# Strassen's seven products for gate and up in a two-layer decoder kernel

## The chip, the cores and the metric

One core of a Trainium2 chip runs the whole program. The time is device microseconds of one execution, the median of the runs. TensorE (PE) multiplies, VectorE (DVE) and ScalarE (ACT) work elementwise, GpSimd (POOL) does small scalars, and SyncE (SP) issues the loads.

## The reference, cut to what matters

Two layers on 256 tokens of width 1024, all in 32-bit floats. Each layer has four sublayers: a gated unit, a mixer with two attentions, a second gated unit, and a gated embedding. The change touches the gated units, four in all:

```python
D_MODEL, SEQ, DEPTH, D_FF = 1024, 256, 2, 2816

def swiglu(x, w_gate, w_up, w_down):
    return (jax.nn.silu(x @ w_gate) * (x @ w_up)) @ w_down

for i in range(DEPTH):
    f = swiglu(rmsnorm(h, g[0]), ffn_gate[i, 0], ffn_up[i, 0], ffn_down[i, 0])
    h = h + 0.5 * rmsnorm(f, g[1])
    # mixer, second gated unit, gated embedding
```

## The kernel before

Every 32-bit product is made of three TensorE matmuls: each operand is split into `hi + lo`, and `hi*hi`, `hi*lo`, `lo*hi` are summed in PSUM (`mm3`). The weight is the moving operand, 512 columns at a time; the 256 tokens are two tiles of 128 (`t`), and a block of their transpose (`xh`, `xl`, 128 x 128) is the stationary one.

`Weights` streams the weights in the order of use. SP loads 1 MB into one of four raw tiles (L131). `prepare` takes a half of it, a piece of 1024 elements per partition: ACT copies it into `hi` (L152), DVE subtracts to get `lo` (L153). The pieces lie in slots: eight, and in the gated units two more that the mixer otherwise uses. `need` prepares a piece on the spot if it isn't there; `finish` gives its slot back when the last matmul that reads it has been emitted. When a raw tile's last piece is split, the next load is emitted.

The engines' queues are in the order in which the program emits. A phase is a generator that yields after every three matmuls or so; `run` puts in the splits (`W.tick`) and other work at the steps that a table, `PLAN`, has for the phase.

A gated unit (`ffn`) goes over `CHUNKS`, six stretches of its 2816 hidden columns, 512 wide and one of 256. In each: gate and up for both tiles (`gate`, `up`; 24 matmuls each at 512 columns), silu on ACT (L448), the product on DVE (L453), transposes and split of the hidden tile (`hid_t`, L398 to L402), and the product with `w_down` (`down`, L479), which sums over all chunks in four PSUM banks (`accs`). The factor of the norm before (`rx`) is put in at silu and product. In the first chunk, what the sublayer before has left over (the rest of its norm and the transposes of x, `pend`) lies between the matmuls; the last chunk ends with the norm after (`begin_post`, `post`).

The bank pool `mm` has four banks, in rotation, for gate, up and the transposes.

Of the kernel before, what the change touches and what calls it, by code (L numbers as in the profile page):

```python
# [17 lines left out]
P = 128  # L18
D = 1024
# [17 lines left out]
NRAW = 4  # L37
CHUNKS = [(0, 512), (512, 512), (1024, 256), (1280, 512), (1792, 512), (2304, 512)]
# [58 lines left out]
class Weights:  # L97
    """Streams the weights in the order of their use: one load per raw tile, which is then
    split into pieces hi + lo = w, each of 12 significant bits."""

    def __init__(self, nc, raw_pool, slots):
        """slots: pairs of (pool, tag, columns) for hi and lo; those of self.shut are taken by others."""
        self.nc, self.raw_pool, self.slots = nc, raw_pool, slots
        self.free = list(range(len(slots)))
        self.shut = set()
        self.slot = {}
        self.specs = []
        self.loads = []
        self.raw = {}
        self.got = {}  # L110
        self.next = 0
        self.next_load = 0

    def add(self, keys, src, a, n):
        load = len(self.loads)
        self.loads.append((src, a * len(keys), n))
        for i, key in enumerate(keys):
            self.specs.append((key, load, i, a, n, i == len(keys) - 1))

    def load_one(self):  # L120
        i = self.next_load
        if i >= len(self.loads):
            return
        src, a, n = self.loads[i]
        raw = self.raw_pool.tile([P, 2048], F32, tag="raw", name=f"raw{i}")
        view = raw[:, : a * n].rearrange("p (a n) -> p a n", n=n)
        if i == 0:
            for j in range(0, a, a // 2):
                self.nc.sync.dma_start(view[:, j : j + a // 2], src[:, j : j + a // 2])
        else:  # L130
            self.nc.sync.dma_start(view, src)  # L131
        self.raw[i] = view
        self.next_load += 1

    def pick(self):
        return next((i for i in self.free if i not in self.shut), None)

    def can(self):
        return self.next < len(self.specs) and self.pick() is not None

    def prepare(self):
        key, load, part, a, n, last = self.specs[self.next]
        while self.next_load <= load:
            self.load_one()
        raw = self.raw[load][:, part * a : (part + 1) * a, :]
        slot = self.pick()
        self.free.remove(slot)
# [3 lines left out]
        hv, lv = (v.rearrange("p (a n) -> p a n", n=n) for v in (hi, lo))  # L151
        self.nc.scalar.activation(hv, raw, AF.Copy)  # L152
        self.nc.vector.tensor_tensor(lv, raw, hv.bitcast(F32), op=ALU.subtract)  # L153
        self.got[key] = (hv, lv)
        self.next += 1
        if last:
            del self.raw[load]
            self.load_one()
# [4 lines left out]

    def need(self, key):
        while key not in self.got:
            assert self.can(), (key, self.specs[self.next])
            self.prepare()
        return self.got[key]

    def finish(self, key):  # L170
        self.free.append(self.slot.pop(key))
        self.free.sort()
# [3 lines left out]
def hybrid_block(ctx: ExitStack, tc: tile.TileContext, a, out):  # L176
# [53 lines left out]
    ones = const.tile([1, P], F32, name="ones")  # L230
    nc.gpsimd.memset(ones, 1.0)

# [1 line left out]
    slots = [((piece_pool, f"hi{i}", 1024), (piece_pool, f"lo{i}", 1024)) for i in range(NS)]  # L234
    slots += [((work, "kdt", 1024), (work, "grp", 1024)), ((work, "vm", T * H * VW), (work, "vd", T * H * VW))]
    W = Weights(nc, raw_pool, slots)
    for l in range(DEPTH):
        for f in range(2):
            if f == 1:
# [3 lines left out]
                def add_in(name, c0, n):  # L243
                    for j in range(2):
                        W.add([(l, name, 2 * j), (l, name, 2 * j + 1)], win[:, 4 * j : 4 * j + 4, c0 : c0 + n], 2, n)

                add_in("A", 0, ZA)
                add_in("dq", ZA, 512)
                W.add([(l, "qu", 0), (l, "qu", 1)], a["w_q_up"][l].rearrange("(k p) n -> p k n", p=P), 1, 768)
                W.add([(l, "kvu", 0)], a["w_kv_up"][l].rearrange("(k p) n -> p k n", p=P), 1, 1024)  # L250
                add_in("dk", ZA + 512, 512)
                add_in("dv", ZA + 1024, 512)
                for half in range(2):
                    for n in range(2):
                        W.add([(l, "wo", half, n, 0), (l, "wo", half, n, 1)],
                              wo[:, 4 * half : 4 * half + 4, n * 512 : (n + 1) * 512], 2, 512)
            wg = a["ffn_gate"][l, f].rearrange("(k p) n -> p k n", p=P)
            wu = a["ffn_up"][l, f].rearrange("(k p) n -> p k n", p=P)
            wd = a["ffn_down"][l, f].rearrange("(k p) n -> p k n", p=P)
            for c, (f0, w) in enumerate(CHUNKS):  # L260
                ka = 1024 // w
                for name, src in (("G", wg), ("U", wu)):
                    for j in range(KD // (2 * ka)):
                        W.add([(l, f, c, name, 2 * j), (l, f, c, name, 2 * j + 1)],
                              src[:, 2 * ka * j : 2 * ka * (j + 1), f0 : f0 + w], ka, w)
                for j in range(w // 256):
                    k0 = f0 // P + 2 * j
                    W.add([(l, f, c, "D", 2 * j), (l, f, c, "D", 2 * j + 1)], wd[:, k0 : k0 + 2, :], 1, 1024)
        gt = a["w_ple_gate"][l].rearrange("(k p) n -> p k n", p=P)
        for n in range(2):  # L270
            for j in range(2):
                W.add([(l, "gt", n, 2 * j), (l, "gt", n, 2 * j + 1)],
# [637 lines left out]
```

## Time and profile before

| | |
|---|---|
| median of 2 runs | 1053.22 us (1052.02 to 1054.42) |
| span of the profiled execution | 1052.4 us |
| PE busy | 1037.1 us, 5168 matmuls |
| DVE busy | 645.8 us, 819 instructions |
| ACT busy | 528.9 us, 744 instructions |
| POOL busy | 51.1 us, 123 instructions |
| bytes moved by DMA | 189.02 MB |

The profiled execution is known by its span, which lies 0.8 us below the median of the runs. Busy time is the time with at least one instruction of the engine under way; waits are listed as "engine line <- releaser: us in total, times, longest". A row of a group ends with its busy time, the mean ns of one, and the idle time before it with what ended it. In the timeline each row begins with start and length.

### The profile page before, as it was taken

How to read it: one execution, taken by the hardware profiler on the slowest of the kernel's cores; microseconds unless marked ns; L12 is line 12 of the kernel's file. 1: busy time of each engine (PE TensorE's matmuls, PEld its weight loads, DVE VectorE, ACT ScalarE, POOL GpSimd, SP SyncE). 2: the span in 40 equal slices, each digit the busy share in tenths (PEclk: the TensorE clock that was granted, in tenths of full speed). 3: DMA queues.
4: the chain of work that ended last, by engine and by line, in shares of the span. 5: the costliest groups of instructions: out<-in, count | busy, mean ns of one | idle time of the engine just before them, and what ended most of it. 6: DMA issues, size and time to landing. Idle time of an engine off the chain costs nothing.

```text
span 1052.4 us, 13069 instructions
## 1 busy us (share of the span) xinstructions
PE 1037.1 (99%) x5168; PEld 867.0 (82%) x5168; DVE 645.8 (61%) x819; ACT 528.9 (50%) x744; POOL 51.1 (5%) x123
## 2 busy tenths in 40 slices
PE   8999999999999999999999999999999999999997
PEld 5889888878888898888878888888888888988886
DVE  4765554778677455456776545557877864555474
ACT  5544443555556444444665444445564654444463
POOL 0000000210020000000110000002000200000011
PEclk9999999999999999999999999999999999999999
DMA  8864546364227564554547645455532575545601
GB/s 321 304 227 168 193 164 211 106 222 160 82 94 272 191 213 160 201 200 160 200 160 259 212 169 200 153 163 168 180 120 82 190 275 184 198 162 172 227 21 40
DMA packets 86158, 189.02 MB, mean 180 GB/s; under 512 B 3665, under 2 KB 15313, under 8 KB 86098
## 3 DMA queue, kind: packets, MB, share of 16 engines
q1 hardware_dynamic: 86098, 188.20, 52.0%
q8 instruction: 40, 0.66, 0.2%
q14 instruction: 20, 0.16, 0.0%
HBM read 187.13 MB, written 1.05 MB: 179 GB/s over the span
## 4 chain that ended last, share of the span: by engine, by line
PE 92%; DVE 3%; ACT 2%; DMA 1%; issue 1%; POOL 0%; SPq 0%; DVEq 0%; POOLq 0%; ACTq 0%
PE acc L479 23%; PE u L323 8%; PE u L321 8%; PE u L322 8%; PE g L321 7%; PE g L323 7%; PE g L322 7%; PE tp L398 3%; PE o L706 2%; PE sc L666 1%; DVE lo L153 1%; PE gt L323 1%; PE gt L322 1%; PE gt L321 1%; PE f L321 1%; PE f L323 1%
## 5 line engine op out<-in xcount | busy, mean ns | idle before, releaser
L153 DVE TENSOR_TENSOR lo<-raw,hi 128x1024 fp32r<-128x1024 f32 (+1 forms) x338 | 405.1, 1214 | 204.2 <-ACT hi L152 194.1
L152 ACT ACTIVATE hi<-raw 128x1024 fp32r<-128x1024 f32 (+1 forms) x338 | 347.2, 1049 | 170.9 <-PE u L323 79.3
L479 PE MATMUL acc<-hi,hid 128*128 128x512 f32 x704 | 201.5, 392 | 0.0
L479 PEld LDWEIGHTS acc<-hi,hid 128*128 128x128 f32 x704 | 131.7, 188 | 27.4
L321 PE MATMUL u<-hi,xh 128*128 128x512 f32 (+1 forms) x384 | 145.3, 379 | 0.0
L323 PE MATMUL u<-hi,xl 128*128 128x512 f32 (+1 forms) x384 | 143.2, 373 | 0.0
L322 PE MATMUL u<-lo,xh 128*128 128x512 f32 (+1 forms) x384 | 143.0, 372 | 0.0
L321 PE MATMUL g<-hi,xh 128*128 128x512 f32 (+1 forms) x360 | 135.0, 375 | 2.3 <-ACT xh L401 2.3
L323 PE MATMUL g<-hi,xl 128*128 128x512 f32 (+1 forms) x360 | 134.6, 374 | 0.0
L322 PE MATMUL g<-lo,xh 128*128 128x512 f32 (+1 forms) x360 | 134.5, 374 | 0.0
L479 PE MATMUL acc<-lo,hid 128*128 128x512 f32 x352 | 118.3, 395 | 0.0
L323 PEld LDWEIGHTS u<-hi,xl 128*128 128x128 f32 x384 | 72.3, 188 | 13.0
L322 PEld LDWEIGHTS u<-lo,xh 128*128 128x128 f32 x384 | 72.4, 188 | 12.1
L321 PEld LDWEIGHTS u<-hi,xh 128*128 128x128 f32 x384 | 72.3, 188 | 12.0
L321 PEld LDWEIGHTS g<-hi,xh 128*128 128x128 f32 x360 | 68.5, 190 | 14.4 <-ACT xh L401 2.7
L322 PEld LDWEIGHTS g<-lo,xh 128*128 128x128 f32 x360 | 68.5, 190 | 12.3 <-DVE lo L153 0.5
L323 PEld LDWEIGHTS g<-hi,xl 128*128 128x128 f32 x360 | 68.4, 190 | 12.4 <-DVE xl L402 0.6
L479 PEld LDWEIGHTS acc<-lo,hid 128*128 128x128 f32 x352 | 66.2, 188 | 13.2
L401 ACT ACTIVATE hid<-tp 128x512 fp32r<-128x512 f32 (+1 forms) x48 | 27.0, 563 | 95.6 <-PE tp L398 95.6
L453 DVE SCALAR_TENSOR_TENSOR hm<-u,rs,silu 128x512 f32<-128x512 f32 (+1 forms) x48 | 33.7, 703 | 65.1 <-PE u L323 65.1
L448 ACT ACTIVATE silu<-g,rs 128x512 f32<-128x512 f32 (+1 forms) x48 | 31.3, 652 | 81.3 <-PE g L323 81.2
L402 DVE TENSOR_TENSOR hid<-tp,hid 128x512 fp32r<-128x512 f32 (+1 forms) x48 | 31.0, 647 | 44.0 <-ACT hid L401 43.6
(216 smaller groups left out, 1195.0 us busy)
## 6 DMA issues: line engine op xcount, KB each, us to landing
raw<-in_ffn_up SPq DMA_DIRECT2D x44, 1024.0 KB, 5.1
raw<-in_ffn_down SPq DMA_DIRECT2D x44, 1024.0 KB, 5.0
raw<-in_ffn_gate SPq DMA_DIRECT2D x43, 1024.0 KB, 5.2
raw<-in_w_in SPq DMA_DIRECT2D x12, 1024.0 KB, 5.2
raw<-in_w_out SPq DMA_DIRECT2D x8, 1024.0 KB, 5.1
raw<-in_w_ple_gate SPq DMA_DIRECT2D x8, 1024.0 KB, 5.1
gain<-in_norm_gains SPq DMA_DIRECT2D x15, 512.0 KB, 4.0
raw<-in_w_in SPq DMA_DIRECT2D x4, 832.0 KB, 5.2
```

What stands on the lines that cost most here:

```text
L152: self.nc.scalar.activation(hv, raw, AF.Copy)
L153: self.nc.vector.tensor_tensor(lv, raw, hv.bitcast(F32), op=ALU.subtract)
L321: nc.tensor.matmul(ps, sh, wh, start=first, stop=False)
L322: nc.tensor.matmul(ps, sh, wl, start=False, stop=False)
L323: nc.tensor.matmul(ps, sl, wh, start=False, stop=last)
L398: nc.tensor.transpose(ps[:, j * P : (j + 1) * P], src[:, (b0 + j) * P : (b0 + j + 1) * P], ident)
L401: nc.scalar.activation(hv, v, AF.Copy)
L402: nc.vector.tensor_tensor(dl[:, k0 + b0 : k0 + b0 + nb, :], v, hv.bitcast(F32), op=ALU.subtract)
L448: nc.scalar.activation(s[:, :w], ps[:, :w], AF.Silu, scale=rx[t][:, 0:1])
L453: nc.vector.scalar_tensor_tensor(hm[:, :w], ps[:, :w], rx[t][:, 0:1], sg[t][:, c0 : c0 + w], op0=ALU.mult, op1=ALU.mult)
L479: nc.tensor.matmul(accs[t][n], hid[t][x][:, b, :], ws[w][:, 0, n * 512 : (n + 1) * 512], start=first and x + w == 0, stop=final and x == 1)
L706: nc.tensor.matmul(dst, pt[:, b * P : (b + 1) * P], va[:, kb, hd, :], start=kb == 0, stop=kb == t)
```

## The change

`CHUNKS` becomes `UNITS`: a plain chunk of 512, a stretch of 1024 ("s"), a plain chunk of 256, a stretch of 1024. In a stretch, gate and up are each a product of a 2 x 2 block matrix of x (two token tiles, two halves of the 1024 inputs) with a 2 x 2 block matrix of the weight (two halves of the inputs, two of the columns), made by Strassen's scheme from seven products of blocks instead of eight.

- On the side of x, which needs the norm's factors inside (`xs`), four sums of blocks are made and split in the first chunk (`scaled`, `sums`, `rescale`), into tiles that the mixer otherwise uses; so the gated units have eight slots.
- On the side of the weight the sums are made in the raw tiles: for P5, P4 and P7 by a DMA from GpSimd that adds to what is in the tile (`then`), for P6 by an add on DVE (`plus`). Each product has two pieces of 1024 elements per partition.
- The products are put together on ACT and DVE (`keep_copy`, `dve`), and where the signs allow, in PSUM (`on=True`).
- A raw tile has 0.5 MB and there are eight.
- In the gated units `flow` and `pump` take the place of `run` and `PLAN`: the planner counts the microseconds of PE and DVE that it has emitted and prepares the next piece of the list when its DVE count is at most 0.5 us ahead of its PE count, at most 5 us ahead of the piece's planned time `at`, and, for a sum by DMA, 8.5 us after its issue. The list is sorted by the planned times.

```diff
-NRAW = 4
-CHUNKS = [(0, 512), (512, 512), (1024, 256), (1280, 512), (1792, 512), (2304, 512)]
+NRAW = 8
+MM = 0.227
+UNITS = [("c", 0, 512), ("s", 512, 1024), ("c", 1536, 256), ("s", 1792, 1024)]
 class Weights:
+    LAND = 8.5
     def prepare(self):
...
+        if plus is not None:
+            self.nc.vector.tensor_tensor(raw, raw, self.raw[self.load_of[plus[0]]], op=ALU.add)
+            self.dve += 1.2
         self.nc.scalar.activation(hv, raw, AF.Copy)
         self.nc.vector.tensor_tensor(lv, raw, hv.bitcast(F32), op=ALU.subtract)
+        self.dve += 1.2
...
+        if then is not None:
+            target, blocks = then
+            self.nc.gpsimd.dma_start(self.raw[self.load_of[target]], blocks, accum_op=ALU.add)
+            self.ready[target] = max(self.pe, self.dve) + self.LAND
...
+    def pump(self, us):
+        self.pe += us
+        self.dve = max(self.dve, self.pe - 1.0)
+        while self.can() and self.dve <= self.pe + 0.5:
+            spec = self.specs[self.next]
+            if spec[7] is not None and (self.pe < spec[7] - 5.0 or self.pe < self.ready.get(spec[4], -99.0)):
+                return
+            self.prepare()
...
+    def ffn_weights(l, f):
...
+            if kind == "c":
+                ka, phase = 1024 // w, 24 * MM * w / 512
...
+                now += 4 * phase + 0.9
+                for j in range(w // P):
+                    todo.append((now + 6 * MM * j - 6, dict(key=(l, f, u, "D", j), ...)))
+                now += 12 * MM * (w // P)
+                continue
+            for name, src in (("G", wg), ("U", wu)):
+                for i in range(2):
...
+                    for dt, prod, load, k, n, plus, then in (
+                        (-17.0, "P1", A, 0, 0, None, (A, block(0, 1))),
+                        (-5.0, "P5", A, 0, 0, None, None),
+                        (-2.5, "P6", A, 0, 0, (B, block(1, 1)), (A, block(1, 0))),
+                        (-1.0, "P3", B, 1, 1, None, (B, block(0, 1))),
+                        (8.5, "P2", C, 1, 0, None, None),
+                        (11.5, "P7", B, 1, 1, None, None),
+                        (14.0, "P4", A, 0, 0, None, None),
+                    ):
+                        todo.append((now + dt + 1.3 * i, dict(key=(l, f, u, name, prod, i), ...)))
+                now += 84 * MM
+            now += 1.0
+            for j in range(8):
+                todo.append((now + 12 * MM * j - 5, dict(key=(l, f, u, "D", (j + 4) % 8), ...)))
+            now += 96 * MM + 0.9
+        for at, spec in sorted(todo, key=lambda x: x[0]):
+            W.add(at=at, **spec)
...
+    def flow(gen, *inserts):
+        inserts = list(inserts)
+        n = 0
+        for us in gen:
+            n += 1
+            while inserts and inserts[0][0] <= n:
+                inserts.pop(0)[1]()
+            W.pump(us)
+        for _, fn in inserts:
+            fn()
...
+        def scaled():
+            rb = bank("rb")
+            dg = k2("dg")
+            for t in range(T):
+                nc.scalar.activation(dg[:, t * P : (t + 1) * P], ident, AF.Copy, scale=rx[t][:, 0:1])
+            for t in range(T):
+                nc.tensor.matmul(rb[:, t * P : (t + 1) * P], ones, dg[:, t * P : (t + 1) * P], start=True, stop=True)
+            for t in range(T):
+                xs[t] = k4("xs").rearrange("p (k q) -> p k q", q=P)
+                nc.vector.tensor_tensor(xs[t], xh[t].bitcast(F32), xl[t].bitcast(F32), op=ALU.add)
+                nc.vector.tensor_tensor(xs[t], xs[t], rb[:, None, t * P : (t + 1) * P].to_broadcast([P, KD, P]), op=ALU.mult)
+            W.dve += 4.9
...
+        def sums():
...
+                nc.vector.tensor_tensor(views[name], i0, i1, op=op)
+                W.dve += 0.7
+                split_x(*S[name], views[name])
+        def rescale(t):
+            split_x(xh[t], xl[t], xs[t])
...
+        def strassen(c):
+            sgs = {}
+            for mat in "GU":
...
+                pa = bank("pa")
+                flow(product(c, mat, "P1", pa))
+                s1 = keep_copy(pa, "s1")
+                pd = bank("pd")
+                flow(product(c, mat, "P5", pd))
+                s5 = keep_copy(pd, "s5")
+                pb = bank("pb")
+                flow(product(c, mat, "P6", pb))
+                u2 = k2("u2")
+                dve(u2, pb, s1, op=ALU.add)
+                flow(product(c, mat, "P3", pd, on=True))
+                dve(s1, pd, u2, op=ALU.subtract)
+                out(0, 1, s1, True)
+                flow(product(c, mat, "P2", pa, on=True))
+                out(0, 0, pa, False)
+                pc = bank("pc")
+                up = mat == "U"
+                flow(product(c, mat, "P7", pc), *([(2, lambda: hid_t(0, sgs[0, 1], 4, hid2))] if up else []))
+                dve(u2, pc, u2, op=ALU.add)
+                dve(s5, s5, u2, op=ALU.subtract)
+                out(1, 1, s5, True)
+                pq = bank("pq")
+                flow(product(c, mat, "P4", pq), *([(2, lambda: hid_t(0, sgs[0, 0], 4))] if up else []))
+                dve(u2, pq, u2, op=ALU.add)
+                out(1, 0, u2, True)
+            hid_t(1, sgs[1, 1], 4, hid2)
+            flow(down_pairs(c, 4, hid2), (2, lambda: hid_t(1, sgs[1, 0], 4)))
...
+            if c == 0 and len(pend) == 3:
+                gate(0, c, (1, pend[0]), lo_last=True)
+                hm0 = up(0, c, (2, pend[1]), (6, pend[2]))
+                gate(1, c, (4, h0), (6, scaled))
+                hm1 = up(1, c, (1, sums), (7, lambda: rescale(0)))
+            elif c == 0:
+                gate(0, c, (7, pend[0]), (7, pend[1]))
+                gate(1, c)
+                hm0 = up(0, c, (1, scaled), (4, sums))
+                hm1 = up(1, c, (6, h0), (7, lambda: rescale(0)))
...
+            flow(down(0, c, nb, 0, False), (5 * nb // 4, h1), (5 * nb // 4, lambda: rescale(1) if c == 0 else None))
+            flow(down(1, c, nb, 0, False))
```

`product` emits the 12 matmuls of a product, three per block, and asks for its two pieces (`W.need`); `down_pairs` emits the product with `w_down` for four blocks of hidden columns, two blocks at a time and both token tiles for each two; `out` is silu on ACT for gate and the product with it on DVE for up.

More of the change, by code (lines that the diff above doesn't have):

```diff
@@ L112, in __init__, with add, plan @@
         self.next_load = 0
[L114 to L118, printed above, removed]
+        self.pe = self.dve = 0.0
+        self.ready = {}
+    def add(self, key, src, a, n, load=None, plus=None, then=None, at=None):
+        self.specs.append((key, src, a, n, load or key, plus, then, at))
+    def plan(self):
+        for key, src, a, n, load, plus, then, at in self.specs:
+            for name, blocks in ((load, src), plus or (None, None)):
+                if name is None:
+                    continue
+                if name not in self.load_of:
+                    self.load_of[name] = len(self.loads)
+                    self.loads.append((blocks, a, n))
+                    self.uses.append(0)
+                self.uses[self.load_of[name]] += 1
@@ L120, in load_one @@
     def load_one(self):
         i = self.next_load
[L122 removed]
+        if i >= len(self.loads) or not self.raw_free:
             return
         src, a, n = self.loads[i]
[L125 removed]
+        slot = self.raw_free.pop(0)
+        raw = self.raw_pool.tile([P, 1024], F32, tag=f"raw{slot}", name=f"raw{i}", bufs=1)
         view = raw[:, : a * n].rearrange("p (a n) -> p a n", n=n)
[L127 to L131, printed above, removed]
@@ L132, in load_one, with used @@
-        self.raw[i] = view
-        self.next_load += 1
-    def pick(self):
-        return next((i for i in self.free if i not in self.shut), None)
+        self.nc.sync.dma_start(view, src)
+        self.raw[i], self.raw_slot[i] = view, slot
+        self.next_load += 1
+    def used(self, load):
+        self.uses[load] -= 1
+        if self.uses[load] == 0:
+            del self.raw[load]
+            self.raw_free.append(self.raw_slot.pop(load))
+            self.load_one()
     def can(self):
-        return self.next < len(self.specs) and self.pick() is not None
+        return self.next < len(self.specs) and bool(self.free)
@@ L141, in prepare @@
     def prepare(self):
-        key, load, part, a, n, last = self.specs[self.next]
-        while self.next_load <= load:
+        key, src, a, n, name, plus, then, at = self.specs[self.next]
+        load = self.load_of[name]
+        last = load if plus is None else max(load, self.load_of[plus[0]])
+        while self.next_load <= last:
+            assert self.raw_free, (key, list(self.raw))
             self.load_one()
-        raw = self.raw[load][:, part * a : (part + 1) * a, :]
-        slot = self.pick()
@@ L147, in prepare @@
-        self.free.remove(slot)
+        raw = self.raw[load]
+        slot = self.free.pop(0)
         self.slot[key] = slot
@@ L237, in hybrid_block, with halves @@
+    def halves(keys, src, a_, n):
+        for i, key in enumerate(keys):
+            W.add(key, src[:, a_ * i : a_ * (i + 1)], a_, n)
     for l in range(DEPTH):
@@ L848, in hybrid_block @@
     for n in range(2):
-        nc.tensor.matmul(gain0[n], ones, row[:, n * 512 : (n + 1) * 512], start=True, stop=True)
+        nc.tensor.matmul(gain0[n], ones[:1], row[:, n * 512 : (n + 1) * 512], start=True, stop=True)
     def enter(t):
```

254 lines of the change are left out of this document (160 added, 94 removed).

## The prediction

> **What bounds the kernel.** I read the page first, then the waits of PE, then stretches of one gated unit, then the timeline at DVE's and PE's pace.
>
> ```profile
> span 1052.4 us, 13069 instructions
> PE 1037.1 (99%) x5168; PEld 867.0 (82%) x5168; DVE 645.8 (61%) x819; ACT 528.9 (50%) x744; POOL 51.1 (5%) x123
> PE 92%; DVE 3%; ACT 2%; DMA 1%; issue 1%; POOL 0%; SPq 0%; DVEq 0%; POOLq 0%; ACTq 0%
> PE g L321 <- ACT xh L401: 2.3, 1, 2.3
> PE gain L849 <- DMA row<-in_norm_gains: 2.2, 1, 2.2
> 339.00 7.56 PE acc L479 x33
> ```
>
> The first line is the span, the second the busy shares, the third the chain that ended last, by engine. PE is busy 99% and carries 92% of the chain; its two longest kinds of wait are 2.3 and 2.2 us in all, both at the start. So the time is the number of matmuls times their pace, and the pace is the last line's: 33 matmuls of 512 columns in 7.56 us, 0.229 us each (the mean of one row, 0.39, is a latency that overlaps the next).
>
> The span is 1052.4 us; the runs' median is 1053.22, so I add 0.8 at the end. What this measurement can tell from no change is about 2%, 21 us: faster is below 1032, slower above 1074.
>
> **What is removed.** Gate and up of a 1024-column stretch were 2 matrices x 2 token tiles x 2 halves x 8 blocks x 3 = 192 matmuls; seven products of 4 blocks x 3 are 84 per matrix, 168. 24 fewer x 2 stretches x 4 gated units = 192 fewer, x 0.229 = **44.0 us**. It all lies on the chain. Added on PE: two 128x128 matmuls per unit for the broadcast of the token factors. The nearest rows are the transposes:
>
> ```profile
> 309.41 0.60 PE L398 MATMUL tp<-ident,xn 128*128 128x128 f32 x4
> 309.76 0.48 PE L321 MATMUL f<-hi,xh 128*128 128x512 f32 x1
> L398 PE MATMUL tp<-ident,hm 128*128 128x128 f32 x176 | 27.0, 272 | 0.0
> ```
>
> Four start within 0.35 us, and one lasts 0.27: between 0.2 and 0.5 us for the two, I take 0.3, 1.2 us in all.
>
> **What is added on DVE.** Each matrix of a stretch needs 14 split pieces of 1024 elements instead of 8, two adds of two raw tiles, and five combinations of banks. What such an instruction costs in a row of them:
>
> ```profile
> 331.46 4.68 DVE L153 TENSOR_TENSOR lo<-raw,hi 128x1024 fp32r<-128x1024 f32 x4 [1.70 <-ACT hi L152]
> 336.06 0.74 DVE L453 SCALAR_TENSOR_TENSOR hm<-u,rs,silu 128x512 f32<-128x512 f32 x1
> 336.72 1.22 DVE L153 TENSOR_TENSOR lo<-raw,hi 128x1024 fp32r<-128x1024 f32 x1
> 308.54 0.69 DVE L381 TENSOR_TENSOR xn<-h,gain 128x512 f32<-128x512 f32 x1
> 309.15 0.74 DVE L379 SCALAR_TENSOR_TENSOR h<-y,rs,h 128x512 f32<-128x512 f32 x1
> L152 ACT ACTIVATE hi<-raw 128x1024 fp32r<-128x1024 f32 x326 | 337.1, 1056 | 159.6 <-PE u L323 68.6 <-PE acc L479 59.2 <-PE g L323 22.3
> L448 ACT ACTIVATE silu<-g,rs 128x512 f32<-128x512 f32 x40 | 27.5, 688 | 72.5 <-PE g L323 72.5
> 300.30 0.63 ACT L354 ACTIVATE junk<-om 128x512 bf16<-128x512 f32 x1 [6.12 <-DVE om L716]
> ```
>
> Four splits take 4.60 us to the next start: 1.15 each. 512 elements take 0.6 (308.54 to 309.15), with a factor per token 0.67 (336.06 to 336.72). ACT's half of a split is 1.06 for 1024, 0.63 for 512 from SBUF, 0.69 for silu. Before, DVE had room beside two plain 512-column chunks:
>
> ```profile
> 398.00:420.00 22.00, 22.00 (x100) 18.21 (x99) 9.90 (x10) 9.48 (x11) 0.00 (x0) 1.00 0.56 186
> 420.00:431.50 11.50, 11.50 (x54) 9.44 (x54) 7.13 (x8) 5.21 (x7) 0.00 (x0) 1.00 0.57 194
> 431.50:453.70 22.20, 22.20 (x101) 18.35 (x100) 10.09 (x10) 9.65 (x11) 0.00 (x0) 1.00 0.54 184
> 453.70:465.00 11.30, 11.30 (x54) 9.30 (x53) 6.93 (x8) 5.16 (x6) 0.00 (x0) 1.00 0.57 198
> ```
>
> (after the times: length, then PE, PEld, DVE, ACT, POOL busy; clock, DMA share, GB/s; rows one and three are gate and up, two and four down.) DVE is busy 20.0 of 44.2 us of gate and up. In the new stretch gate and up take PE 168 x 0.229 = 38.5 us, and DVE has 28 splits and 4 adds, 32 x 1.15 = 36.8, ten combinations and four products with silu, 14 x 0.6 = 8.4, and two splits of the hidden, 1.2: **46.4 us of DVE beside 38.5 of PE**. Each add stands in front of its own split in DVE's queue, with ACT's half between, so DVE also waits 4 x 1.06 = 4.2. ACT itself has 28 x 1.06 + 4 copies x 0.6 + 4 silu x 0.7, about 35: below PE. So in these 38.5 us DVE is the longer engine, and the eight slots of pieces are its only lead: P1, P5 and P6 of gate before the stretch begins are 6 splits, 2 adds and 2 waits, 11.3 us. 46.4 + 4.2 - 11.3 + 1.15 for the first down piece = 40.4 against 38.5 and 0.7 of transposes: 1.2 us late even if DVE never waits for PE. That is the lower bound per stretch.
>
> It does wait, by the order in the queues. The planner emits a piece only when its count of DVE is at most 0.5 us ahead of its count of PE, with 1.2 per split and 0.7 per combination. In gate's 19.2 us it has 12 splits and 5 combinations, 17.9, so up's P6 (2 x 2.4) comes at up's start, and up's P3 pieces some 5.5 and 6.8 us into up, not 1 us ahead of it as its list wants. On the chip DVE then has 2 x (1.15 + 1.06 + 1.15) = 6.7 us for P6 and 1.15 for P3: P3's raw tile is free for its accumulating DMA at about 8 us, and P7 is due after five products, 60 x 0.229 = 13.7. The transfer and ACT's half have 5.7 us.
>
> No row shows an accumulating DMA. The nearest are plain ones of its size:
>
> ```profile
> raw<-in_ffn_up SPq DMA_DIRECT2D x44, 1024.0 KB, 5.1
> raw<-in_w_kv_up SPq DMA_DIRECT2D x2, 512.0 KB, 3.6
> grp<-in_group_out_norm SPq DMA_DIRECT2D x2, 512.0 KB, 5.9
> h<-in_x SPq DMA_DIRECT2D x2, 512.0 KB, 7.0
> 335.00:346.50 11.50, 11.50 (x54) 9.48 (x53) 8.61 (x9) 6.74 (x7) 0.00 (x0) 1.00 0.94 343
> ```
>
> 3.6 us is the lower end; 14, twice the slowest (it must also read the sum's tile), the upper. The stretch moves 32 blocks of 0.524 MB in some 62 us, 270 GB/s where it was 24 in 67 (187, as the windows show); by the last row 0.94 of the engines goes with 343, so 0.74 or more. Under that load I take 7.0, the loaded row: 7.0 + 1.06 - 5.7 = 2.4, I say **2.0 us** late at up's P7. By the Trainium skill's page "DMA: Bandwidth & Descriptors" (section "Anatomy of one DMA — SWDGE (gpsimd) path") a DMA issued by GpSimd takes about 2.0 us and its bytes over 436 GB/s; an estimate by it is 3.2 us for 0.5 MB, with no wait here and a sum 16 us lower; no run here shows such a DMA.
>
> Next is P4. Its second half is emitted when it is needed, behind three combinations that wait for P7's last matmul, and behind the first down piece, which the sorted list puts ahead of it: 3 x 0.6 + 2 x 1.15 = 4.1 us against PE's first half, 6 matmuls, 1.4. 2.7 late, I take **2.5**. The DMAs' issue on POOL costs nothing beside this: POOL is 5% busy and its chain (the norm's factors) lies in other stages, and SP's loads wait for DVE as before. 4.5 us per stretch (1.2 to 11, the upper with a 14 us transfer) x 8 = **36 us**. In the down phase (96 matmuls, 22 us) DVE has 8 splits and 2 hidden splits, 10.4, and catches up.
>
> **The first chunk of each unit.** It keeps its 144 matmuls but carries the scaled tokens (4 of 1024: 4.6 us), the four sums (add, ACT, split: 0.6 + 0.63 + 0.6 = 1.83 each, 7.3), and the first rescale (1.15). Where the unit follows the mixer or the last sublayer, all eight slots hold gate's and up's pieces until the second gate phase frees them at its steps 2, 4, 6; the list's order there is P1, D0, P1, D1 (planned at 16.6, 16.7, 17.9, 18.1). Two are emitted before step 6 puts in the scaled tokens; after that the planner's DVE count (4.9, then 5.6) blocks the rest until a matmul asks. So D1 stands behind scaled, sums, rescale, hm and a P1 split: from 15.0 us (step 6, 66 matmuls), 4.6 + 7.3 + 1.15 + 0.67 + 2 x 1.15 = 16.0, ready at 31.0; PE comes to it after 96 + 6 matmuls, 23.4 us. **7.6 us late.** In the unit at the program's start the same work stands ahead of hm0 and D0, for much the same. Bounds: 2 us, if the planner gets the down pieces out first, and 8.5. 4 x 7.6 = **30 us**. The eight slots (ten before) matter by this: PE's cover was pieces split ahead.
>
> Mixer and gate of the last sublayer run the same steps on the same eight slots; their first pieces may come 1 us earlier or later, which I leave at 0.
>
> **Sum.** 1052.4 - 44.0 + 1.2 + 36 + 30 = 1075.6, and 0.8: **1076 us**, +2.2%.
>
> **Rivals.** *PE keeps going* (the other side): DVE's excess is swallowed by the lead, as the queues run asynchronously and DVE's 61% leaves 400 us. Then only the lower bounds stay, 8 x 1.2 + 4 x 2 = 18: 1053.2 - 44.0 + 1.2 + 18 = 1028. It decides at a loss per stretch under 2 us with the first chunk under 2.5. For it: PE hardly waited on any of the 326 whole pieces of before; against it: that was at 20 of 44 us. *One of the two stalls is absent:* without the first chunk's (2 instead of 7.6) 1054, without the stretches' (1.2 for 4.5) 1050: within 2%. *The sums land late:* at 10.5 us instead of 7.0 each stretch loses 3.5 more, 28: 1104; for it, the 0.94 share above, against it 5.1 us of median landing for twice the bytes. *PE is slow after its wait:*
>
> ```profile
> 10.17 0.79 PE L321 MATMUL g<-hi,xh 128*128 128x512 f32 x1 [2.28 <-ACT xh L401]
> 12.14 0.63 PE L321 MATMUL g<-hi,xh 128*128 128x512 f32 x1
> 12.57 0.63 PE L322 MATMUL g<-lo,xh 128*128 128x512 f32 x1
> 15.55 0.63 PE L323 MATMUL g<-hi,xl 128*128 128x512 f32 x1
> 15.98 0.60 PE L321 MATMUL g<-hi,xh 128*128 128x512 f32 x1
> 12.00:16.00 4.00, 4.00 (x11) 3.03 (x11) 3.50 (x5) 2.00 (x2) 0.00 (x0) 1.00 1.04 388
> ```
>
> After a first wait of 2.28 us, 12 matmuls took 5.81 us up to 15.98, 0.48 each, 3.1 more than at 0.229. If each 7.6 us stall is followed by such a stretch, 4 x 3.1 = 12: 1088. It is not in the sum because in this row PE had not yet been fast. The Trainium skill's "TensorE: Matmul & The Clock Gate" (section "Part 1: The HAM clock gate") says that an idle window of about 3.4 us halves the clock and as much work brings it back; the start agrees by pace, 0.43 us from 12.14 to 12.57, though the granted clock of this stretch reads 1.00 in the last row.
>
> That the change doesn't do what it says is hardly open for the matmuls, which the code fixes; for the order of pieces it is the second rival.
>
> **Chances.** Forecast 0.40 (its own range 1062 to 1092, 0.23 of the 0.40 above 1074), PE keeps going 0.24, one stall absent 0.16, late sums 0.10, slow after a wait 0.10. Slower: 0.23 + 0.20 = 0.43; faster 0.21 (0.03 of that rival lies above 1032); within 2% 0.36. The range leaves out the lower part of the fast rival and the upper of the late sums: 1026 to 1106.
>
> **What would show it.** PE's instruction count falls by some 180. Right: DVE above 80%, PE's waits no longer a few us but 50 to 70, on lo and hi of down pieces in each unit's first down phase, and in each stretch on up's P7 (ACT waiting for a DMA) and P4. Wrong, to the fast side: PE's waits under 25 us. Wrong, to the slow side: DMA share near 1 in gate and up, ACT waiting on the pool queue in both matrices, or matmuls of 0.43 us after a stall.

## The result, and the profile after

The changed kernel takes **1517.37 us** (1516.84 to 1517.89, two runs) against 1053.22: a ratio of 1.441 (95% interval 1.437 to 1.445). It is 464 us slower, where 1076 us and a range up to 1106 were forecast. From the page of the changed kernel, the span, the busy shares, the granted clock by slices, and the chain that ended last:

```profile
span 1515.1 us, 13985 instructions
PE 1195.9 (79%) x4992; PEld 910.4 (60%) x4992; DVE 892.2 (59%) x1083; ACT 641.8 (42%) x904; POOL 173.7 (11%) x219
PEclk9768898999998779888987779988899987799899
PE 42%; DVE 20%; issue 19%; ACT 9%; DMA 7%; POOL 2%; SPq 0%; ACTq 0%; DVEq 0%; POOLq 0%
```

No engine is a bound: PE is busy 79%, DVE only 59%. PE's own share of the chain fell from 92% to 42%, and the rest goes in turn to DVE, ACT, DMA and "issue". PE's idle time rose from 15.3 to 319.2 us. It also does 176 matmuls fewer in 159 us more, and the clock, 9 in every slice before (90% or more), falls to 7 and 6: its matmuls themselves became slow. 304 more idle and 159 more busy make up the whole loss. What PE waits for (engine, tile and line <- releaser: us in total, times, longest):

```profile
PE pq L643 <- ACT hi L177: 44.5, 16, 3.8
PE pq L643 <- DVE lo L178: 35.1, 24, 3.1
PE pc L643 <- ACT hi L177: 33.6, 19, 4.0
PE acc L562 <- ACT hi L177: 32.6, 12, 7.1
PE pa L643 <- DVE lo L178: 23.5, 16, 2.4
PE pc L643 <- DVE lo L178: 20.8, 24, 1.7
PE pd L643 <- DVE lo L178: 18.2, 19, 1.7
PE pb L643 <- DVE lo L178: 17.0, 25, 0.8
```

Every product of the scheme is in the list, of both matrices: P1 and P2 (`pa`), P5 and P3 (`pd`), P6 (`pb`), P7 (`pc`), P4 (`pq`). Each of these waits is for the split of the matmul's own weight piece (`acc` is the down phase). Gate and up of the two stretches of one unit, from the first matmul of P1 to the first of the down phase (after the times: length, PE, PEld, DVE, ACT, POOL busy with counts; clock, DMA share, GB/s):

```profile
473.70:570.50 96.80, 61.70 (x182) 41.19 (x180) 45.22 (x45) 31.00 (x36) 12.07 (x10) 0.79 0.55 124
613.50:691.10 77.60, 54.86 (x182) 38.36 (x180) 44.88 (x45) 29.97 (x35) 12.13 (x10) 0.82 0.64 154
```

They take 96.8 and 77.6 us, where the prediction has 38.5 for PE and 4.5 of waits; the other units' first stretches lie between 94.8 and 96.9, their second ones between 76.1 and 77.6. All eight together take 694 us. DVE's work is there as forecast, 45 us, but it fills only about half of the time, and the DMA share is no wall either. Something orders the engines one after the other. The timeline shows it where the first stretch's second product runs (selected rows; start, length, engine, instruction; in brackets the idle time ahead of it and its releaser):

```profile
476.20 0.39 PE L643 MATMUL pa<-hi,xl 128*128 128x512 f32 x1
476.62 0.60 ACT L651 ACTIVATE s<-pa 128x512 f32<-128x512 f32 x1 [11.50 <-PE pa L643]
477.12 1.05 ACT L177 ACTIVATE hi<-raw 128x1024 fp32r<-128x1024 f32 x1
478.22 0.50 PE L643 MATMUL pd<-hi,sP 128*128 128x512 f32 x1 [0.27 <-ACT hi L177]
478.20 1.22 DVE L178 TENSOR_TENSOR lo<-raw,hi 128x1024 fp32r<-128x1024 f32 x1 [11.45 <-ACT hi L177]
479.48 0.50 PE L643 MATMUL pd<-lo,sP 128*128 128x512 f32 x1 [0.76 <-DVE lo L178]
479.34 1.22 DVE L175 TENSOR_TENSOR raw<-raw,raw 128x1024 f32<-128x1024 f32 x1
480.66 1.06 ACT L177 ACTIVATE hi<-raw 128x1024 fp32r<-128x1024 f32 x1 [2.49 <-DVE raw L175]
481.76 0.50 PE L643 MATMUL pb<-hi,sP 128*128 128x512 f32 x1 [0.85 <-ACT hi L177]
```

Read it from the top. P1's last matmul ends, ACT copies P1 out (`s`, the copy waited 11.50 us for it), and only behind that copy in ACT's queue stands the split of P5's second piece. DVE, idle for 11.45 us, then makes its `lo`, PE gets it, and so on to P6. ACT and DVE had over 11 us to prepare these pieces ahead; their instructions simply stood behind an instruction that waits for PE. So a product runs through a loop PE, ACT, DVE, PE.

The cause is in `pump`. It emits a piece ahead only if the planner's DVE count is at most 0.5 us ahead of its PE count. Gate and up cost the planner 49.5 us of DVE (32 splits and adds at 1.2, 14 combinations at 0.7, two hidden splits at 0.65) beside 38.1 of PE (168 x 0.227), so its DVE count runs ahead and a piece comes late or only from `need`, when the matmul that reads it is next. Followed through the program, which needs no measured time, 95 of the 112 pieces of the four first stretches come from `need`, and 30 of 112 in the second ones; there half of the pieces are emitted at most 1.4 us of PE's work before their matmul, less than ACT's and DVE's halves of one split (1.06 and 1.15 us). P7's pieces have no lead at all in either. The real DVE idles meanwhile, but the planner's counts know no waits.

### The profile page after: what moved, and what is told of

The parts are those of the page before. It is cut to its first block, busy times and chain, and to the rows that moved or that the text cites. A ratio compares the mean times of both kernels' runs of the same rounds, so it can differ in the third digit from the quotient of the medians.

```text
span 1515.1 us, 13985 instructions
## 1 busy us (share of the span) xinstructions
PE 1195.9 (79%) x4992; PEld 910.4 (60%) x4992; DVE 892.2 (59%) x1083; ACT 641.8 (42%) x904; POOL 173.7 (11%) x219
## 3 DMA queue, kind: packets, MB, share of 16 engines
q1 hardware_dynamic: 80066, 171.43, 33.8%
q0 software_dynamic: 26112, 50.34, 19.9%
## 4 chain that ended last, share of the span: by engine, by line
PE 42%; DVE 20%; issue 19%; ACT 9%; DMA 7%; POOL 2%; SPq 0%; ACTq 0%; DVEq 0%; POOLq 0%
DVE lo L178 11%; PE acc L562 8%; ACT hi L177 6%; PE pa L643 4%; PE pq L643 4%; PE pc L643 4%; DMA raw<-in_ffn_up 3%; DMA raw<-in_ffn_gate 2%; PE tp L486 2%; PE pd L643 2%; DVE raw L175 2%; POOL raw L184 1%; PE o L932 1%; PE pb L643 1%; DVE u L655 1%
## 5 line engine op out<-in xcount | busy, mean ns | idle before, releaser
L178 DVE TENSOR_TENSOR lo<-raw,hi 128x1024 fp32r<-128x1024 f32 (+2 forms) x434 | 512.5, 1215 | 248.3 <-ACT hi L177 247.8
L177 ACT ACTIVATE hi<-raw 128x1024 fp32r<-128x1024 f32 (+2 forms) x434 | 432.3, 1044 | 159.3 <-DVE raw L175 66.0
L562 PE MATMUL acc<-hi,hid 128*128 128x512 f32 x448 | 145.7, 428 | 32.2 <-ACT hi L177 32.2
L184 POOL DMA_DIRECT2D raw<-in_ffn_gate x48 | 58.3, 1225 | 512.5 <-DVE lo L178 511.6
L643 PE MATMUL pd<-hi,sP 128*128 128x512 f32 x256 | 90.8, 412 | 2.6 <-ACT hi L177 1.9
L184 POOL DMA_DIRECT2D raw<-in_ffn_up x48 | 58.4, 1238 | 276.7 <-DVE lo L178 275.0
L643 PE MATMUL pc<-hi,sP 128*128 128x512 f32 x128 | 60.3, 529 | 33.7 <-ACT hi L177 33.6
L643 PE MATMUL pa<-lo,xh 128*128 128x512 f32 x128 | 59.5, 465 | 23.6 <-DVE lo L178 23.5
L643 PE MATMUL pq<-hi,xh 128*128 128x512 f32 x64 | 38.9, 607 | 44.5 <-ACT hi L177 44.5
L643 PE MATMUL pa<-hi,xh 128*128 128x512 f32 x128 | 59.2, 462 | 17.1 <-ACT hi L177 17.1
L643 PE MATMUL pq<-lo,xh 128*128 128x512 f32 x64 | 41.1, 642 | 35.1 <-DVE lo L178 35.1
L643 PE MATMUL pa<-hi,xl 128*128 128x512 f32 x128 | 56.5, 442 | 0.0
```

Source lines behind the costliest of these rows:

```text
L184: self.nc.gpsimd.dma_start(self.raw[self.load_of[target]], blocks, accum_op=ALU.add)
L562: nc.tensor.matmul(accs[t][n], hs[t][x][:, b, :], ws[w][:, 0, n * 512 : (n + 1) * 512], start=first and x + w == 0, stop=final and x == 1)
L643: nc.tensor.matmul(ps, x[:, k, :], w[:, j, :], start=not on and k + m == 0, stop=k == 3 and m == 2, skip_group_check=on)
```

## Experiments

All edits are on the changed kernel. Single runs are compared across differences of tens of us; the kernel before took 1052.26 to 1055.41 beside them.

**1. The planner's lead** (`lead`).

```diff
-        while self.can() and self.dve <= self.pe + 0.5:
+        while self.can() and self.dve <= self.pe + 60.0:
```

> The planner may run 60 us ahead in its DVE count instead of 0.5, so that a piece is emitted as soon as a slot is free and its planned time is near; nothing else changes. Theory order (pieces are emitted only when a matmul asks for them, behind copies and combinations that wait for PE, and PE cools in the waits): most of the added time goes, 1070 to 1200 us, and the granted clock is back above 0.95. Theory work (DVE and ACT have too much to do beside the seven products): under 5% less than 1517, above 1440. Theory landing (the accumulating DMAs come too late): under 5% less.

Measured: 1337.38 us, granted clock 0.913. Time and clock both miss what theory order had asked for (1070 to 1200, above 0.95), but the other two theories, above 1440, are further off. One constant, no work changed, gives back 180 us. This shows that the order in the queues, not the engines' work, is the largest single part of the loss. The planner now emits half of the pieces at least 6.1 and 5.4 us of PE's work ahead (first and second stretches); P7's still come from `need`, 30 of 32.

**2. The landing** (`plain`): the pool queue's DMAs overwrite instead of adding, so the weight sums of P5, P4 and P7 are left out.

```diff
-            self.nc.gpsimd.dma_start(self.raw[self.load_of[target]], blocks, accum_op=ALU.add)
+            self.nc.gpsimd.dma_start(self.raw[self.load_of[target]], blocks)
```

> The 96 DMAs of the sums overwrite the raw tile instead of adding to it (so the sums of weights are left out); order, sizes and queues stay. Theory landing: they land in half the 7 us and the time falls by over 10%, below 1370. Theories order and work: within 4% of 1517.

Measured: 1499.04 us, 18 less (1.2%), within the 4% of theories order and work. The DMA rows (tile <- source, queue, count, KB, median us from issue to landing), first of the changed kernel, then of this one:

```profile
raw<-in_ffn_gate POOLq DMA_DIRECT2D x48, 512.0 KB, 7.0
raw<-in_ffn_up POOLq DMA_DIRECT2D x48, 512.0 KB, 7.2
```

```profile
raw<-in_ffn_gate POOLq DMA_DIRECT2D x48, 512.0 KB, 4.2
raw<-in_ffn_up POOLq DMA_DIRECT2D x48, 512.0 KB, 4.6
```

The adding DMA is some 2.7 us slower, and in this order that is worth 2.3 us per stretch. The edit takes out only what adding costs over overwriting; the landing of a plain DMA stays.

**3. The frame without the products** (`chunks`, `chunks_bare`): all six stretches as plain chunks, under the new planner with its eight slots; in the second also without the scaled tokens and their sums.

```diff
-UNITS = [("c", 0, 512), ("s", 512, 1024), ("c", 1536, 256), ("s", 1792, 1024)]
+UNITS = [("c", 0, 512), ("c", 512, 512), ("c", 1024, 256), ("c", 1280, 512), ("c", 1792, 512), ("c", 2304, 512)]
...
-                gate(1, c, (4, h0), (6, scaled))
-                hm1 = up(1, c, (1, sums), (7, lambda: rescale(0)))
+                gate(1, c, (4, h0))
+                hm1 = up(1, c)
```

(The last four lines are in the second kernel alone, with the same edit in the other branch and for `rescale(1)`; the norm's factors go back into silu and product.)

> The new kernel with six plain chunks as before and no stretch by Strassen's scheme; scaled tokens and sums are still made in the first chunk, and the planner, the 0.5 MB tiles and the eight slots stay. It tells what the frame costs without the seven products. Theory order: only the first chunk is late, some 15 us in each of four units as in the trace (52 against 35), so 1100 to 1125. Theory work: 1080 to 1095 (7.6 us per unit). If the frame itself is bad: above 1150.

> The same with scaled, sums and rescale taken out too (the factor of the norm goes in at silu and product again). All theories: within 2% of 1053, 1045 to 1075; anything above 1080 is the price of planner, 0.5 MB loads and eight slots.

Measured: 1133.77 us (ratio to before 1.077, 1.075 to 1.079) and 1075.47 us (1.022, 1.020 to 1.024). Both lie above their ranges, by 9 and 0.5 us. So the frame costs 22 us, the sums in the first chunks 58, 14.6 per unit. The busy row and PE's waits on the down pieces in the first of the two kernels, then the second one's busy row:

```profile
PE 1067.1 (94%) x5184; PEld 878.5 (78%) x5184; DVE 684.2 (60%) x875; ACT 529.9 (47%) x776; POOL 62.0 (5%) x123
PE acc L562 <- ACT hi L177: 20.6, 8, 4.7
PE acc L562 <- DVE lo L178: 5.3, 8, 0.9
```

```profile
PE 1041.3 (97%) x5168; PEld 866.9 (81%) x5168; DVE 638.3 (59%) x819; ACT 514.3 (48%) x744; POOL 63.0 (6%) x123
```

The waits on the down pieces are 25.9 us; PE's busy time rises by 25.8 for 16 small matmuls. So the second half of the 58 us is most likely the pace after the wait: the granted clock is 0.974 in the first kernel and 0.995 in the second. Against `chunks` the products alone lose 384 us where they should have won 44.

**4. The planner's guess of the landing** (`lead_noready`, `lead_pe`). With the lead of 60 the planner's DVE count runs ahead, and `ready` is counted from the larger of the two counts.

```diff
-    LAND = 8.5
+    LAND = -100.0
```

> On top of the 60 us of lead, the planner no longer holds a piece back until its guess of the landing (8.5 us behind the larger of its two counts, and the DVE count now runs far ahead); the chip's own waits on the DMA stay. Theory order: P7 and P4, whose pieces this guess still kept until a matmul asked, come as early as the slots allow, and the waits on pc and pq (108 us in lead) fall by more than half: 1180 to 1270 against 1337. Theory work: within 3% of 1337.

In `lead_pe` the guess stays but is counted from PE: `self.ready[target] = self.pe + self.LAND`.

> Lead of 60 us as before, and the guess of the landing is kept, but from the planner's PE count (8.5 us behind the issue in matmul time) and not from the DVE count that runs ahead. If it pays to emit a piece a landing's length behind its sum (ACT then doesn't stand before a DMA, 83 us of waits without the guess), 1150 to 1215; if pieces come later than slots allow again, above 1260; without the guess it was 1234.

Measured: 1234.37 and 1235.2 us. Another 103 us go, as theory order had it, and both remedies are worth the same; 1235.2 lies between the two ranges of its own expectation. The guess had held back pieces, above all P7's: now no piece of a product comes from `need`, half are emitted at least 9.5 and 8.9 us of PE's work ahead, and the waits on pc and pq fall from 108 to 34 us. Busy row and the longest wait of PE without the guess, and gate and up of one stretch:

```profile
PE 1065.7 (86%) x4992; PEld 854.6 (69%) x4992; DVE 882.2 (72%) x1083; ACT 645.1 (52%) x904; POOL 180.0 (15%) x219
PE pd L643 <- ACT s L651: 36.6, 9, 5.5
404.30:463.10 58.80, 45.34 (x182) 34.34 (x180) 41.88 (x43) 31.15 (x36) 12.17 (x10) 0.94 0.88 213
```

The lo and hi of products are gone from the head of the list. The first wait is now P3, which adds onto P5's bank and waits until ACT has copied it out. A stretch's gate and up take 55.5 to 60.2 us.

**5. Four attempts to order better still.** `lead_noready_at` emits up to 30 us ahead of the planned time (`spec[7] - 30.0`); `c0late` moves the sums behind the down phase's split and `c0split` spreads them over its steps, both with shifted planned times; `s5dve` copies P5 out on DVE instead of ACT. All start from `lead_noready`.

```diff
-            if spec[7] is not None and (self.pe < spec[7] - 5.0 or self.pe < self.ready.get(spec[4], -99.0)):
+            if spec[7] is not None and (self.pe < spec[7] - 30.0 or self.pe < self.ready.get(spec[4], -99.0)):
...
-            flow(down(0, c, nb, 0, False), (5 * nb // 4, h1), (5 * nb // 4, lambda: rescale(1) if c == 0 else None))
+            flow(down(0, c, nb, 0, False), (5 * nb // 4, h1), (5 * nb // 4, lambda: (rescale(1), sums()) if c == 0 else None))
...
-                s5 = keep_copy(pd, "s5")
+                s5 = k2("s5")
+                nc.vector.tensor_copy(s5, pd)
```

> The same, and a piece may come 30 us ahead of its planned time instead of 5. Theory order, if the eight slots are the limit and not the planned times: within 2% of the run without the planned times' limit loosened. If the times still hold pieces back: 3% or more faster than that run.

> As the run with lead and without the landing guess, and the first chunk's pieces in another order: down pieces ahead of P1's, and the sums after the hidden tile's split in the down phase instead of in up. The forecast's step for the first chunk (D1 stands behind scaled and sums) says 30 to 60 us faster than without that; if the burst only moves to the next stretch: within 2%.

> The run without the guess (1234), with the first chunk's down pieces ahead of P1's in the list, hidden split ahead of the sums, and the sums in the first down phase. Step of the forecast for the first chunk: 25 to 45 us faster; if the sums only move into the next stretch, as when they stood a little later (1278): 1234 to 1290.

> The run without the guess (1234), with P5's copy out of its bank on DVE instead of ACT, where it stood behind splits that wait for a landing (PE waited 36.6 us for it ahead of P3). Theory queue (what hurts is the place behind a blocked instruction, not the work): 15 to 40 us faster. If DVE's work is the limit, 0.6 us x 16 more of it: not faster.

Measured: 1282.04, 1277.75, 1235.12 and 1237.94 us: two are slower, two the same. None came out as hoped; `c0split` lies at the edge of its second range, `s5dve` is not faster, and `lead_noready_at` and `c0late` lost 48 and 43 us, which neither of their theories had. In `lead_noready_at` PE's wait for P5's copy grew most, from 36.6 us to this:

```profile
PE pd L643 <- ACT s L651: 87.9, 9, 10.9
```

Its eight longest cases, 9.1 to 10.9 us, are P3 of up in each of the eight stretches. One of them, in ACT's queue and then on PE:

```profile
738.70 1.06 ACT L177 ACTIVATE hi<-raw 128x1024 fp32r<-128x1024 f32 x1 [1.13 <-DMA raw<-in_ffn_up]
741.39 1.06 ACT L177 ACTIVATE hi<-raw 128x1024 fp32r<-128x1024 f32 x1 [1.63 <-DMA raw<-in_ffn_up]
742.35 0.58 ACT L651 ACTIVATE s<-pd 128x512 f32<-128x512 f32 x1
742.98 0.79 PE L643 MATMUL pd<-hi,sP 128*128 128x512 f32 x1 [10.66 <-ACT s L651]
```

Emitted too early, a split stands in ACT's queue until its sum has landed, and the copy of P5, which PE needs first, stands behind it. Too early costs too. In `c0late` ACT waits 93.8 us for DMAs of gate, nearly all of them adding ones (34.2 in `lead_noready`):

```profile
ACT hi L177 <- DMA raw<-in_ffn_gate: 93.8, 22, 10.6
```

In `s5dve` the wait for P5's copy only changed its engine; on DVE it stands behind a split that waits for ACT's half:

```profile
PE pd L643 <- DVE s L680: 30.5, 11, 6.3
```

**6. The clock** (`warm`): on the changed kernel, eight discarded matmuls ahead of P5, P6, P7 and P4, 512 in all.

```diff
+            if not on and name != "P1":
+                for _ in range(8):
+                    nc.tensor.matmul(ps, xh[0][:, 0, :], xh[0][:, 4:8, :].rearrange("p k q -> p (k q)"), start=True, stop=True)
```

> The kernel after, with eight more matmuls of 512 columns, whose result is thrown away, ahead of each of P5, P6, P7 and P4: 512 matmuls, 117 us of PE at full pace, in places where PE mostly waits. Theory clock (the short waits make PE slow and the slow matmuls lengthen every step): the granted clock rises from 0.874 to above 0.93 and the time falls in spite of the added work, 1350 to 1490. If the clock only shows the waits and costs little: 1517 to 1640.

Measured: 1499.15 us, 18 less (1.2%, one run) with some 117 us of matmuls more (512 x 0.229); granted clock 0.907 instead of 0.874. Both theories miss: the first wanted 1350 to 1490 and a clock above 0.93, the second 1517 or more. But PE's busy time rises by only 67 us (1195.9 to 1262.6) and its idle time falls by 84 (319.2 to 234.8), so the pace after waits costs something; the loop itself stays.

**7. What is left at the loosened order** (`lead_noready_plain`, `nolo`, `nolo_plain`, all from `lead_noready`, 1234 us): overwriting DMAs as in 2; no lo split for the 224 pieces of the products (`whole`; their matmuls read hi twice); both.

```diff
-        self.nc.vector.tensor_tensor(lv, raw, hv.bitcast(F32), op=ALU.subtract)
+        if whole:
+            lv = hv
+        else:
+            self.nc.vector.tensor_tensor(lv, raw, hv.bitcast(F32), op=ALU.subtract)
```

> The run without the guess (1234), with the 96 DMAs overwriting instead of adding (sums of weights left out); they land in 4.4 us instead of 6.7. In the kernel after this was worth 18 us of 1517. Theory landing, second form (once the order is loosened the landing is what ACT stands before): 60 us or more faster, below 1175. If the order alone is the limit: 1205 to 1234.

> The loosened order (planner's lead 60 us, no guess of the landing; 1234 us), and the 224 pieces of the products without their split on DVE: the matmuls that should read lo read hi instead, so the rounding part of the gate and up weights is left out and replaced by a second hi. PE's matmuls and all DMAs stay. Theory A (what is left of the stretches' loss is DVE's work and the chain through it, add, ACT's half, split): 224 x 1.15 = 258 us of DVE go, PE's waits on lo and hi of the products vanish almost, time 1120 to 1160 with the clock above 0.98. Rival B (the landing of the accumulating DMA alone sets what is left, 53 us by the run without sums): ACT then waits for the same DMAs, and the time falls by less than 40 us, above 1195.

> As the run before, and the pool queue's DMAs overwrite instead of adding (sums of P5, P4 and P7 left out). Both suspects gone: if they are all of the remaining loss of the stretches, the time is that of the plain chunks with the sums (1134) less the 44 us of matmuls, 1090 to 1105. If it stays above 1130, a third cause is open (ACT's queue, the banks).

Measured: 1181.38, 1166.01 and 1089.85 us. The first lies between its two ranges, 6 us above theory landing's 1175; `nolo` missed the top of theory A by 6 us, and its clock of 0.964 the 0.98; `nolo_plain` met its number. The last one's busy row and longest wait of PE, and gate and up of one stretch:

```profile
PE 1022.5 (94%) x4992; PEld 843.4 (78%) x4992; DVE 626.4 (58%) x859; ACT 644.5 (59%) x904; POOL 132.8 (12%) x219
PE acc L567 <- ACT hi L179: 15.9, 5, 5.2
366.10:405.70 39.60, 39.60 (x181) 32.62 (x180) 14.91 (x19) 29.29 (x34) 5.78 (x8) 1.00 0.91 314
```

No wait of a product is left: PE is busy without a gap in all eight stretches, 39.6 us each, so the four banks do not hold them up. 1089.85 is `chunks` less 44: the 192 removed matmuls are there at last. Adding instead of overwriting costs 53 us beside the splits and 76 without them, the splits 68 beside the adding and 92 without it; together 145. That is 18 us per stretch.

What makes adding dear is not settled. It is a later landing, and it is more work for the DMA engines: by the pages 96 adding DMAs took 19.9% of the engines' 1515.1 us, 3.1 us each for all sixteen, 96 overwriting ones in `plain` 10.9% of 1497.3, 1.7 us. A stretch has 12 of them and 20 loads, which by the changed kernel's page took 1.6 us each (33.8% for 171.43 MB); that makes some 69 us by estimate, where PE has 62 with the down phase. In `nolo`, gate and up of a stretch:

```profile
384.90:434.50 49.60, 42.55 (x182) 33.49 (x180) 14.12 (x18) 29.00 (x34) 10.29 (x9) 0.97 0.97 240
```

There DVE has little left to do, and it is the DMA engines that are busy throughout.

**8. Half of the splits on another engine** (`lopool`, from `lead_noready`): the second piece of each product has its lo made on POOL.

```diff
-        self.nc.vector.tensor_tensor(lv, raw, hv.bitcast(F32), op=ALU.subtract)
+        odd = len(key) == 6 and key[5] == 1
+        (self.nc.gpsimd if odd else self.nc.vector).tensor_tensor(lv, raw, hv.bitcast(F32), op=ALU.subtract)
```

> The loosened order (1234 us), and the second piece of each product has its lo made on POOL instead of DVE: 112 subtractions. Theory A (DVE's work in the chain): the two pieces of a product are split side by side, DVE loses 129 us of work; if POOL takes under 2.4 us for one the time falls to 1190 to 1215. Rival (POOL is slower, or holds up its own DMA issues that stand behind the subtraction): no gain or a loss, 1230 to 1300, with PE's waits on lo from POOL in the list.

Measured: 1298.0 us, 64 slower, as the rival had it. POOL's row, and the wait it makes:

```profile
L179 POOL TENSOR_TENSOR lo<-raw,hi 128x1024 fp32r<-128x1024 f32 x112 | 305.1, 2735 | 234.8 <-ACT hi L177 223.3 <-issue 9.9 <-DMA raw<-in_ffn_up 1.6
PE pa L644 <- POOL lo L179: 43.5, 8, 6.3
```

2.7 us for one, against 1.15 on DVE: the slower half sets when a product can go on. DVE's own splits beside it became slower too, 1.49 us in the mean against 1.22 in `lead_noready`; the two effects are not separated.

No version here beats the kernel before; the best that computes everything is `chunks_bare`, without the scheme, then `chunks` and `lead_noready`.

## Why the prediction was wrong, point by point

The runs form a chain from the kernel before to the one after: 1053 + 22 (frame) + 58 (sums) - 44 (matmuls) + 145 (adding and splits) + 103 (guess) + 180 (lead) = 1517. Each term is a difference of two neighbours, so the sum must come out and proves nothing by itself. The steps interact, and the terms hold for this order of taking them away; the guess, for one, was removed only beside the longer lead.

- **Removed matmuls, 44.0 us: right.** 5168 - 192 + 16 is the count after; the broadcasts are 16 records, not the 8 I counted, and 1134 to 1090 shows the price.
- **The stretches, 36 us: the step that failed**; they lost 427 (384 + 44), most of it in gate and up, 694 us instead of 8 x 38.5. The prediction quotes the planner's rule, but uses it only to delay P6 and P3 of up by a few us, lets each stretch begin with P1, P5 and P6 of gate in the slots (11.3 us of lead) and lets the down phase catch up. In the program only P1 is emitted by the start of a first stretch. From P6 on the planner's DVE count is ahead of its PE count, by some 2 us there and 12 at the end of up, and a count that is ahead emits nothing early; it knows no stall, so the chip's idle DVE doesn't bring it back. All products of both matrices pay, not only up's P7 and P4. The waits on P4 alone are 44.5 + 35.1 = 79.6 us, 5.0 for each of 16 products, where 2.5 was priced for 8 of them. Lead and guess, 283 us, come from this one step.
- **DVE as the longer engine: right as work, wrong as the limit.** DVE is busy 45 us in a stretch's gate and up, against 46.4 forecast, but these take 96.8 and 77.6 us. In the loosened order it is still busy only 41.9 of 58.8. There splits and adding cost 18 us per stretch instead of 4.5.
- **The landing, 7.0 us: right in size** (7.0 and 7.2). The 2.3 us per stretch of `plain` beside the 2.0 predicted is luck: it is the price of adding over overwriting in an order that hides most of it, not P7's delay. What the prediction mis-sized is the load on the DMA engines: it took an adding DMA's bytes at the price of plain ones, 0.74 of the engines over the stretch. The Trainium skill's estimate of 3.2 us from "DMA: Bandwidth & Descriptors" ("Anatomy of one DMA — SWDGE (gpsimd) path") lies below even the overwriting DMA here, 4.2 to 4.6.
- **The first chunks, 30 us: the mechanism right, the size off.** Waits of 25.9 us on down pieces in `chunks` are near it, and the longest in the changed kernel is 7.1 us, where 7.6 was forecast; the 25.8 us of PE's busy time behind them, the slow pace, were a rival, at 12.
- **PE slow after its wait: wrongly kept out of the sum.** "In this row PE had not yet been fast" was the reason. PE that had been fast falls too. From `lead`, PE's timeline:

```profile
457.36 0.40 PE L643 MATMUL pq<-lo,xh 128*128 128x512 f32 x1
457.60 0.39 PE L643 MATMUL pq<-hi,xl 128*128 128x512 f32 x1
460.41 0.80 PE L643 MATMUL pq<-hi,xh 128*128 128x512 f32 x1 [2.42 <-ACT hi L177]
461.86 0.80 PE L643 MATMUL pq<-lo,xh 128*128 128x512 f32 x1 [0.65 <-DVE lo L178]
462.45 0.63 PE L643 MATMUL pq<-hi,xl 128*128 128x512 f32 x1
...
466.72 0.53 PE L643 MATMUL pa<-hi,xh 128*128 128x512 f32 x1
467.09 0.39 PE L643 MATMUL pa<-lo,xh 128*128 128x512 f32 x1
```

Start to start 0.23 us before the waits, 0.43 from 462.45 to 466.72 (ten matmuls), 0.23 after 467.09. The granted clock shows when. In all traces of this case it is full or half and changes only on a grid of 3.41 us. Three intervals of this one, between changes (columns as in the windows above):

```profile
456.77:460.19 3.42, 1.22 (x6) 0.66 (x4) 1.75 (x3) 2.35 (x3) 0.00 (x0) 1.00 1.05 407
460.19:467.01 6.82, 5.95 (x13) 4.38 (x14) 2.31 (x3) 0.80 (x2) 0.00 (x0) 0.50 0.27 89
467.01:470.42 3.41, 3.14 (x13) 2.10 (x12) 0.42 (x1) 1.54 (x2) 0.00 (x0) 1.00 0.00 0
```

After a step in which PE was busy 1.22 of 3.41 us the clock is half, and after one in which PE was busy throughout it is full again. The fall, at 460.19, comes before the second wait: the first was enough. "TensorE: Matmul & The Clock Gate" of the Trainium skill (section "Part 1: The HAM clock gate") puts the limit at an idle window of about 3.4 us; here the step need not be idle. In the changed kernel's trace the clock falls 61 times, always after a step in which PE was busy 0.55 of the time or less by the profile, and it stays full after 267 steps with 0.46 or more. It was half for 382.5 us, in which PE was busy 292.7. At 0.23 us instead of 0.43 that work would take about half as long, so by this estimate the clock accounts for some 146 us of PE's busy time. (The 1.00 in the prediction's last window is no measurement: that trace has no clock record ahead of 16.43 us, where the pace changes.)
- **Mixer and gate, 0 us: wrong** by the 22 us of `chunks_bare`, which has neither products nor sums. Which of planner, slots and raw tiles it is stays open.
- **What would show it.** "DVE above 80%" (59%) and "50 to 70 us of PE's waits" (319.2 idle) failed. ACT's wait for a DMA on up came (62.1 us, against 10.6 on gate), and so did a sign of the slow side, matmuls of 0.43 us after a stall.

How much of the changed kernel's 464 us would go with the clock alone is not settled: the 146 us are an account of one trace, and `warm`, 1.2% faster in one run, left the loop in place.

## What to carry to other kernels

A planner that counts time to decide when to emit must be read with stalls in it: ask what its counts say after the first wait, and whether it then emits anything ahead of need. Work that PE needs next must not stand in a queue behind an instruction that waits, be it for what PE has just made or for a transfer; an engine at 59% can still be late for every product. Saving matmuls by adding pieces pays only if preparing the added pieces hides behind the matmuls that are left: here the products without lo splits and with overwriting DMAs gave the 44 us, and splits and adding cost 145 even in the best order that was found.

## What the runs showed of the hardware

- An accumulating 0.5 MB DMA issued by POOL lands in 7.0 to 7.2 us (medians of the changed kernel; 5.8 to 11.6 in the other runs), an overwriting one in 4.2 to 4.6 (`plain`; 4.3 to 5.7 in the two others). The first takes 3.1 us of all DMA engines, the second 1.7 (by the shares of experiment 7). POOL itself is taken for 1.2 us by the first and 0.7 by the second:

```profile
L184 POOL DMA_DIRECT2D raw<-in_ffn_gate x48 | 58.3, 1225 | 512.5 <-DVE lo L178 511.6 <-issue 0.9
```

```profile
L184 POOL DMA_DIRECT2D raw<-in_ffn_gate x48 | 35.2, 733 | 527.6 <-DVE lo L178 527.6
```

- A PE that ran at 0.23 us per matmul went to 0.43 after a wait of 2.42 us, for some six us. The granted clock was full or half, changed on a grid of 3.41 us, and in the changed kernel fell only after steps in which PE was busy 0.55 of the time or less.
- POOL subtracts 128 x 1024 in 2.7 us, where DVE takes 1.15; beside it DVE's own subtractions took 1.49 us in the mean instead of 1.22.
